# Moving a gate's Silu behind its reload, and loading the Ln/Exp table once for each series of norms

## The chip, the core and the metric

The kernel runs on one core of a Trainium2 chip. The core has five engines, each with its own queue of instructions that it works in order: TensorE (PE in the profile, its weight loads PEld) for matmuls, VectorE (DVE) and ScalarE (ACT) for elementwise work, GpSimd (POOL), and SyncE (SP), which here only issues DMAs. They meet at semaphores. The metric is the device time of one execution in microseconds; the time shown for a kernel is the median of its runs.

## The reference

One layer of a hybrid decoder on x of 1024 tokens by 1024 channels, all in float32: a SwiGLU feed-forward half-step (ffn1), a mixer of three branches (a gated recurrence, sliding-window attention, attention into 256 memory tokens), merged by sigmoid gates and projected, and a second half-step (ffn2). Each has an RMS norm on its input and one on its output.

```python
def rms_norm(x, g):
    xf = x.astype(jnp.float32)
    y = xf * lax.rsqrt(jnp.mean(xf * xf, axis=-1, keepdims=True) + NORM_EPS)
    return (y * g.astype(jnp.float32)).astype(x.dtype)

def swiglu(u, w_in, w_out):
    gate, up = jnp.split(u @ w_in, 2, axis=-1)
    return (jax.nn.silu(gate) * up) @ w_out

f1 = swiglu(rms_norm(h, ffn1_pre_g[l]), ffn1_w_in[l], ffn1_w_out[l])
h = h + HALF_STEP * rms_norm(f1, ffn1_post_g[l])
u = rms_norm(h, mix_pre_g[l])
...
h = h + rms_norm(merged @ w_out[l], mix_post_g[l])
f2 = swiglu(rms_norm(h, ffn2_pre_g[l]), ffn2_w_in[l], ffn2_w_out[l])
h = h + HALF_STEP * rms_norm(f2, ffn2_post_g[l])
```

D_FF is 2816, so gate and up have 22 blocks of 128 columns each.

## The kernel before

**Layout.** Channels lie on the 128 partitions, tokens along the free dimension, in two halves of 512. A float32 operand of a matmul is cut into a high part (a cast, on ACT) and a low part (a subtraction, on DVE), and each product is three matmuls (`mm3`, lines 330 to 332). `split` does this for activations (lines 410 and 411), `operand` for weights (264 and 266). Weights come in strips of 256 KB through five buffers (`w_raw`); eight cut operands (`w_hi`, `w_lo`) are kept ahead of PE.

**Feed-forward input.** The two matrix products are done by a scheme with seven products of quarters of x instead of eight, with seven factors made from them. Two of these factors, `b11` and `b21`, are made from the first half of the tokens alone. So work can begin before the second half is ready:

- the gate phase: for the first 9 blocks of ffn1 and the first 13 of ffn2, `ffn_in_gate` makes the two products with `b11` and `b21`: `px` is copied to `m1` by ACT (line 578), `py` is added to it by DVE (582), and the sum goes through Silu on ACT (583). `m1` and the result `g0` are stored to DRAM (`first_d`, lines 535 and 536).
- beside it, the norm of the second half and the factors made from it (`factors_part`, `factors_end`: lines 498 to 518). In ffn2 this begins with the output norm of the projection, then the input norm of ffn2.
- the pairs (`ffn_in_pair`): for each of the 22 blocks the other five products, with `t2`, `t1`, `t3`, `b22`, `t4`. For the blocks that were begun ahead (called `rest`), `m1` and `g0` are reloaded (595 and 596); the first product `px` plus `m1` gives `u1` (604) and then `px` goes on collecting the third and the fifth product in the same PSUM bank. DVE adds `m1` (625) and multiplies `g0` by the result (626). For the other blocks (called `pair`) `ffn_in_gate` runs inside. Each pair has one more Silu of its own, for the second half of the tokens (621). After each block DVE also makes sums of output weights (552 to 555) and forms of the hidden values (564 to 567), which are stored.

**The norm.** `inverse_root` takes the sum of squares and adds eps while it cuts it in two (`sq_hi` on ACT at 393, `sq_lo` on DVE at 394), loads the table set that holds Ln and Exp (395), lets PE take the mean over the channels (397), and makes the inverse root by Ln (400), Exp (401) and one Newton step: Square on ACT (402), two operations on DVE (403 and 404). It is called 13 times: twice for ffn1's input, four times behind ffn1's output (output norm and mixer norm for each half), four times behind the projection (output norm and ffn2's input norm for each half), and three times at the end (the last half in two pieces).

**Tables.** [...] Silu is not in the set of Ln and Exp. The load at 395 is written out. All others are put in at compile time before an instruction whose function isn't in the set loaded at that point. Casts, copies and Square need no particular set.

**What sets the order.** The queues are filled by a planner that simulates the program: on each engine it takes, among what it holds to be ready, what has the highest priority, which is the order of the program unless `high_priority` moves it up (by `lead` 300 or `urgent` 1000 instructions). `keep` (`keep_in_program_order`) pins an instruction behind the one traced before it on its engine. Once planned, the order on each engine is fixed, and an instruction that waits holds all behind it.

Of the kernel before, what the change touches and what calls it, by code (L numbers as in the profile page):

```python
# [14 lines left out]
ACT = mybir.ActivationFunctionType  # L15
# [192 lines left out]
class Builder:  # L208
# [175 lines left out]
    def inverse_root(self, sq, pool, between=None):  # L384

        nc = self.nc
        n = sq.shape[1]
        hi, lo, y = (pool.tile([P, n], t, tag=f"sq{n}", name=name, bufs=4) for t, name in ((F32R, "sq_hi"), (F32R, "sq_lo"), (F32, "rs")))
        ps = self.psum("ps_rs")[:, :n]
        V, S = nc.vector, nc.scalar  # L390
        keep = self.tc.keep_in_program_order
        with self.tc.high_priority(offset=self.lead):
            keep(S.activation(hi, sq, ACT.Identity, bias=self.eps))
            V.scalar_tensor_tensor(lo, sq, self.eps, hi.bitcast(F32), ALU.add, ALU.subtract)
            keep(S.preload_act_table_set("natural_log_exp_and_others"))
            for i, x in enumerate((hi, lo)):
                mm = nc.tensor.matmul(ps, self.mean_r, x, start=i == 0, stop=i == 1)
                if between:
                    keep(mm)
            keep(S.activation(y, ps, ACT.Ln))  # L400
            keep(S.activation(y, y, ACT.Exp, scale=-0.5))
            keep(S.activation(sq, y, ACT.Square))
            V.scalar_tensor_tensor(sq, ps, -0.5, sq, ALU.mult, ALU.mult)
            V.scalar_tensor_tensor(y, sq, 1.5, y, ALU.add, ALU.mult)
        if between:
            between()
        return y
# [80 lines left out]
    def quarters(self, xs):  # L488
        return ([xs[k + a][h] for k in range(KH)] for h in (0, 1) for a in (0, KH))
# [32 lines left out]
    def ffn_in(self, f, x, form_d, first_d, parts, norm):  # L522

        nc, V = self.nc, self.nc.vector
        with self.tc.tile_pool(reuse_waits="tile", name="ffn_in", bufs=2) as pool:
            self.sums = pool
            self.factors_begin(pool)
            for part in parts:
                norm(part, pool)
                self.factors_part(x, part, pool)  # L530
            self.factors_end(x)

            for j in range(FIRST[f]):
                px, m1, g0 = self.ffn_in_gate(f + "_gate", j, pool)
                nc.sync.dma_start(first_d[j, 0], m1)
                nc.sync.dma_start(first_d[j, 1], g0)
            stored = None
            for i in range(KP):
                *first, made = self.ffn_in_pair(f, 2 * i, pool, first_d)
                self.out_sums(f, i, pool, stored or self.reload, made)  # L540
                *second, _ = self.ffn_in_pair(f, 2 * i + 1, pool, first_d)
                stored = self.out_forms(i, first, second, pool, form_d)
# [26 lines left out]
            stored = nc.sync.dma_start(form_d[B_FORM[n], i], t)  # L569
        return stored  # L570

    def ffn_in_gate(self, name, j, pool):
        nc, fs = self.nc, self.fs
        px, py = self.psum("px"), self.psum("py")
        self.product(px, self.take(name, j), fs["b11"], True)
        x = pool.tile([P, TH], F32, tag="px", name="m1", bufs=3)
        with self.tc.high_priority(offset=self.urgent):
            nc.scalar.copy(x, px)
        self.product(py, self.take(name, j), fs["b21"], True, True)
        g = pool.tile([P, TH], F32, tag="gate", name="g", bufs=6)  # L580
        with self.tc.high_priority(offset=self.urgent):
            nc.vector.tensor_tensor(g, py, x, ALU.add)
        nc.scalar.activation(g, g, ACT.Silu)
        return px, x, g

    def ffn_in_pair(self, f, j, pool, first_d):
        nc, fs = self.nc, self.fs
        V = nc.vector
        ahead = j < FIRST[f]
        name = f + ("_rest" if ahead else "_pair")  # L590
        if ahead:
            px = self.psum("px")
            m1 = pool.tile([P, TH], F32, tag="m1", name="m1", bufs=2)
            g0 = pool.tile([P, TH], F32, tag="gate", name="g", bufs=6)
            self.reload = nc.sync.dma_start(m1, first_d[j, 0])
            nc.sync.dma_start(g0, first_d[j, 1])
        else:
            px, _, g0 = self.ffn_in_gate(name, j, pool)

        def out(ps, what):  # L600
            t = pool.tile([P, TH], F32, tag="px", name=what, bufs=3)
            with self.tc.high_priority(offset=self.lead):
                if ahead:
                    V.tensor_tensor(t, ps, m1, ALU.add)  # L604
                else:
                    nc.scalar.copy(t, ps)
            return t

        pz = self.psum("pz")
        self.product(px, self.take(name, j), fs["t2"], ahead)  # L610
        x = out(px, "u1")
        self.product(pz, self.take(name, j), fs["t1"], True)
        z = out(pz, "m5")
        self.product(px, self.take(name, j), fs["t3"])
        up = pool.tile([P, TH], F32, tag="up", name="up", bufs=2)
        with self.tc.high_priority(offset=self.lead):
            V.tensor_tensor(up, px, z, ALU.add)
        self.product(pz, self.take(name, j), fs["b22"], last=True)
        g1 = pool.tile([P, TH], F32, tag="gate", name="g", bufs=6)
        V.tensor_tensor(g1, pz, x, ALU.add)  # L620
        nc.scalar.activation(g1, g1, ACT.Silu)
        V.tensor_tensor(g1, g1, up, ALU.mult)
        self.product(px, self.take(name, j), fs["t4"], last=True)
        if ahead:
            V.tensor_tensor(m1, m1, px, ALU.add)
            made = V.tensor_tensor(g0, g0, m1, ALU.mult)
        else:
            made = V.tensor_tensor(g0, g0, px, ALU.mult)
        return g0, g1, made
# [915 lines left out]
    def build(self):  # L1545
        nc, tc, io = self.nc, self.tc, self.io
        with contextlib.ExitStack() as outer, tc.tile_pool(reuse_waits="tile", name="consts", bufs=1) as cp, \
             tc.tile_pool(reuse_waits="tile", name="w", bufs=1) as self.wpool, \
             tc.tile_pool(reuse_waits="tile", name="pmm", bufs=8, space=bass.MemoryType.PSUM) as self.pmm:
            self.sum_d = {f: tc.dram_tile([len(SUMS), KP, P, KH, P], F32, name=f + "_sum_d") for f in ("ffn1", "ffn2")}  # L1550
            self.plan()
            self.vecs = cp.tile([P, NVEC], F32, name="vecs")
            nc.scalar.dma_start(self.vecs, io["vecs"])
            self.ones = cp.tile([P, 1], F32, name="ones")
# [40 lines left out]
                    self.mixer_first(u, pool, att_d)  # L1595
            mixed = self.mixer(u, mixc, raws.close, att_d, gate_d, km_d, vm_d)
            consts.close()
            with quarters() as self.qpool:
                merged = self.last_branches(*mixed)
                x = self.acc_tiles()  # L1600
                projection = self.out_projection(merged, x)
                post = lambda part, xr, pool: self.post_norm(x, part, lambda k: self.vec("mix_post_g", k), xr, pool, h2)
                part = next(projection)
                with tc.tile_pool(reuse_waits="tile", name="out_proj", bufs=2) as pool:
                    post(part, self.residual(h1, part, self.res_tile), pool)
                    xr = self.residual(h1, HALVES[1], lambda: self.u_tile(F32))
                    self.factors_norm(x, part, "ffn2_pre_g", pool)
                    self.factors_first(x)

                def ready(part, pool):  # L1610
                    post(part, [t[:, part[1] : part[2]] for t in xr], pool)
                    self.factors_norm(x, part, "ffn2_pre_g", pool)

                self.ffn_in("ffn2", x, form_d, first_d, projection, ready)
                with tc.tile_pool(reuse_waits="tile", name="ffn_out", bufs=2) as pool, \
                     tc.tile_pool(reuse_waits="tile", name="keep", bufs=OPS) as self.keep, \
                     tc.tile_pool(reuse_waits="tile", name="forms", bufs=8) as self.forms:
                    acc = self.new_u()
                    for part in self.ffn_outs("ffn2", form_d, acc):
                        xr = self.residual(h2, part, self.res_tile)  # L1620
                        self.post_norm(acc, part, lambda k: self.post2[:, k : k + 1], xr, pool, io["out"])
# [69 lines left out]
```

## Time and profile before

| | |
|---|---|
| median of 3 runs | 2321.53 us (2320.19 to 2323.29) |
| profiled execution, its own time | 2316.22 us |
| span from first to last instruction | 2314.5 us |
| mean granted PE clock | 0.994 of full speed |
| table loads on ACT at line 395 | 13, of 1283 ns |
| table loads on ACT at line 583 | 5, of 1283 ns |
| Silu at line 583, at line 621 | 44 and 44, of about 632 ns |

A row of a group gives line, engine, operation, output and inputs by name, shapes and count; then busy time in us, mean ns of one, the engine's idle time just before them, and who ended it. A row of a timeline begins with start and duration in us. A row of the waits gives who waited for whom, the total, how often, and the longest. The lines of the functions quoted above are those of the profile.

### The profile page before, as it was taken

The page shows a single profiled execution, that of the slowest core. Times are in us where ns is not written, and L with a number is a line of the kernel's source. Part 1 is how long each engine was busy: PE and PEld are TensorE (multiplying, and loading weights), DVE is VectorE, ACT ScalarE, POOL GpSimd, SP SyncE. Part 2 cuts the span into 40 slices and gives each one's busy share as a digit, 9 for nine tenths or more (in the row PEclk, how much of TensorE's full clock was granted, in tenths as well). Part 3 has the DMA queues.
Part 4 walks back from the last instruction along what each step waited for, and adds up shares of the span by engine and source line. Part 5 has one row for each costly group of instructions (what it writes and reads, how often), then busy time and mean ns, then how long its engine had stood idle before and what let it go on. Part 6 is the DMA issues. An engine that isn't in the chain of part 4 may idle for free. (4 is left out here: it accounts for less than half of the span.)

```text
span 2314.5 us, 33492 instructions
## 1 busy us (share of the span) xinstructions
PE 2263.2 (98%) x11914; PEld 1847.6 (80%) x11914; DVE 1656.0 (72%) x2683; ACT 1008.1 (44%) x1856; POOL 94.9 (4%) x134
## 2 busy tenths in 40 slices
PE   8999999999999999999999999999989999999997
PEld 6778888888888777888878877878868778888887
DVE  6998666665698786995645466575899886666576
ACT  6522333454566553223444454235762223345452
POOL 0000000000000000001300000340000000000000
PEclk9999999999999999999999999999999999999999
DMA  7477544586644447325445334554456774557663
GB/s 271 166 264 249 178 150 168 170 293 201 192 164 156 108 119 193 121 96 180 142 139 176 122 108 151 189 176 168 167 188 233 260 249 167 169 189 268 207 192 118
DMA packets 280776, 417.68 MB, mean 180 GB/s; under 512 B 82304, under 2 KB 104320, under 8 KB 280352
## 3 DMA queue, kind: packets, MB, share of 16 engines
q1 hardware_dynamic: 231552, 388.20, 50.6%
q10 hardware_dynamic: 49056, 27.34, 4.3%
q8 instruction: 94, 1.54, 0.3%
q14 instruction: 74, 0.61, 0.1%
HBM read 284.89 MB, written 129.50 MB: 179 GB/s over the span
## 5 line engine op out<-in xcount | busy, mean ns | idle before, releaser
L264 ACT CAST w_hi<-w_raw 128x512 fp32r<-128x512 f32 x594 | 365.5, 619 | 732.7 <-PE px L331 138.4
L266 DVE TENSOR_TENSOR w_lo<-w_raw,w_hi 128x512 fp32r<-128x512 f32 x594 | 413.6, 699 | 219.3 <-ACT w_hi L264 196.1
L331 PE MATMUL po<-u,w_hi 128*128 128x512 f32 (+1 forms) x476 | 181.0, 380 | 0.0
L330 PE MATMUL po<-u,w_hi 128*128 128x512 f32 (+1 forms) x476 | 181.0, 380 | 0.0
L332 PE MATMUL po<-u,w_lo 128*128 128x512 f32 (+1 forms) x476 | 181.0, 380 | 0.0
L330 PE MATMUL pgate<-u,w_hi 128*128 128x512 f32 x384 | 155.5, 405 | 0.0
L332 PE MATMUL pgate<-u,w_lo 128*128 128x512 f32 x384 | 151.3, 394 | 0.0
L330 PE MATMUL px<-f,w_hi 128*128 128x512 f32 x352 | 139.6, 397 | 11.4 <-DVE u L604 8.6
L331 PE MATMUL pgate<-u,w_hi 128*128 128x512 f32 x384 | 149.8, 390 | 0.0
L330 PE MATMUL px<-u,w_hi 128*128 128x512 f32 x352 | 137.5, 391 | 4.5 <-ACT w_hi L264 2.3
L331 PE MATMUL px<-f,w_hi 128*128 128x512 f32 x352 | 138.2, 393 | 0.3 <-DVE f L411 0.2
L332 PE MATMUL px<-f,w_lo 128*128 128x512 f32 x352 | 137.9, 392 | 0.0
L331 PE MATMUL px<-u,w_hi 128*128 128x512 f32 x352 | 137.0, 390 | 0.8 <-DVE u L411 0.8
L330 PE MATMUL pz<-u,w_hi 128*128 128x512 f32 x352 | 137.1, 390 | 0.2 <-DVE m L604 0.2
L331 PE MATMUL pz<-u,w_hi 128*128 128x512 f32 x352 | 137.2, 390 | 0.0
L332 PE MATMUL px<-u,w_lo 128*128 128x512 f32 x352 | 137.0, 389 | 0.0
L332 PE MATMUL pz<-u,w_lo 128*128 128x512 f32 x352 | 137.0, 389 | 0.0
L411 DVE TENSOR_TENSOR u<-hid,u 128x512 fp32r<-128x512 f32 x114 | 78.3, 689 | 45.2 <-ACT u L410 44.4
L331 PEld LDWEIGHTS po<-u,w_hi 128*128 128x128 f32 x476 | 89.5, 188 | 17.1
L330 PEld LDWEIGHTS po<-u,w_hi 128*128 128x128 f32 x476 | 89.5, 188 | 17.1
L332 PEld LDWEIGHTS po<-u,w_lo 128*128 128x128 f32 x476 | 89.5, 188 | 16.9
L410 ACT CAST u<-hid 128x512 fp32r<-128x512 f32 x114 | 70.7, 620 | 64.9 <-DMA hid<-form_d 56.5
(357 smaller groups left out, 5149.7 us busy)
## 6 DMA issues: line engine op xcount, KB each, us to landing
w_raw<-in_ffn_in SPq DMA_DIRECT2D x220, 256.0 KB
hid<-form_d SPq DMA_DIRECT2D x154, 256.0 KB
w_raw<-in_win SPq DMA_DIRECT2D x112, 256.0 KB
ws<-in_ffn_out SPq DMA_DIRECT2D x88, 256.0 KB
form_d<-g SPq DMA_DIRECT2D x88, 256.0 KB
ffn_sum_d<-ws SPq DMA_DIRECT2D x88, 256.0 KB
w_raw<-ffn_sum_d SPq DMA_DIRECT2D x88, 256.0 KB
form_d<-h SPq DMA_DIRECT2D x66, 256.0 KB
```

Of the source, the lines that this page charges most:

```text
L264: self.nc.scalar.copy(hi, x)
L266: self.nc.vector.tensor_tensor(lo, x, hi.bitcast(F32), ALU.subtract)
L330: mm(out, wh, xh, start=first, stop=False, **kw)
L331: mm(out, wh, xl, start=False, stop=False, **kw)
L332: mm(out, wl, xh, start=False, stop=last, **kw)
L410: self.nc.scalar.copy(hi, x)
L411: self.nc.vector.tensor_tensor(lo, x, hi.bitcast(F32), ALU.subtract)
```

## The change

Two things change. First, the Silu of the blocks begun ahead is no longer made in the gate phase. What is stored in `first_d` is the gate before Silu, and the Silu is made on `g0` after its reload, after the operand of the fifth product has been taken. For the other blocks nothing changes.

Second, a flag `log_table` says whether the set of Ln and Exp has been loaded for the running series of norms. `inverse_root` loads it only if the flag is not set, ahead of `sq_hi` instead of behind it, and sets the flag. The flag is cleared at the start, before the pairs of each feed-forward, and before the last branches of the mixer.

```diff
@@ inverse_root
         with self.tc.high_priority(offset=self.lead):
+            if not self.log_table:
+                keep(S.preload_act_table_set("natural_log_exp_and_others"))
+                self.log_table = True
             keep(S.activation(hi, sq, ACT.Identity, bias=self.eps))
             V.scalar_tensor_tensor(lo, sq, self.eps, hi.bitcast(F32), ALU.add, ALU.subtract)
-            keep(S.preload_act_table_set("natural_log_exp_and_others"))
@@ ffn_in
             for j in range(FIRST[f]):
-                px, m1, g0 = self.ffn_in_gate(f + "_gate", j, pool)
+                px, m1, g0 = self.ffn_in_gate(f + "_gate", j, pool, True)
                 nc.sync.dma_start(first_d[j, 0], m1)
                 nc.sync.dma_start(first_d[j, 1], g0)
             stored = None
+            self.log_table = False
             for i in range(KP):
@@ ffn_in_gate
-    def ffn_in_gate(self, name, j, pool):
+    def ffn_in_gate(self, name, j, pool, early=False):
...
-        nc.scalar.activation(g, g, ACT.Silu)
+        if not early:
+            nc.scalar.activation(g, g, ACT.Silu)
@@ ffn_in_pair
         self.product(px, self.take(name, j), fs["t4"], last=True)
         if ahead:
+            nc.scalar.activation(g0, g0, ACT.Silu)
             V.tensor_tensor(m1, m1, px, ALU.add)
@@ build
             self.plan()
+            self.log_table = False
...
             consts.close()
+            self.log_table = False
             with quarters() as self.qpool:
                 merged = self.last_branches(*mixed)
```

## The prediction

> **What bounds the kernel now.** I read the page first, then the list of who kept TensorE (PE) waiting, then busy times by stretch, and last the timelines of ScalarE (ACT) and VectorE (DVE) around the longest wait. The page's line of engines:
>
> ```profile
> PE 2263.2 (98%) x11914; PEld 1847.6 (80%) x11914; DVE 1656.0 (72%) x2683; ACT 1008.1 (44%) x1856; POOL 94.9 (4%) x134
> ```
>
> PE is busy nearly throughout, so ACT time as such is worth nothing; only places where PE waits can pay. The first of PE's waits (total, times, longest):
>
> ```profile
> PE px L330 <- DVE u L604: 8.6, 2, 8.3
> ```
>
> The one of 8.3 us stands out: a matmul of the third product of the first pair of ffn2 waits for DVE to read the PSUM bank (`u` at L604). Busy times by stretch, in the order PE, PEld, DVE, ACT, POOL, then granted clock, DMA share and GB/s:
>
> ```profile
> 93.00:112.00 19.00, 16.41 (x62) 10.71 (x61) 18.88 (x33) 9.28 (x18) 0.00 (x0) 1.00 0.47 157
> 830.60:834.00 3.40, 0.19 (x1) 0.00 (x0) 0.69 (x1) 2.10 (x4) 0.00 (x0) 1.00 1.04 199
> 835.80:838.80 3.00, 3.00 (x9) 2.33 (x8) 2.74 (x3) 1.36 (x2) 0.00 (x0) 0.50 0.30 119
> ...
> 1691.00:1699.00 8.00, 8.00 (x36) 6.36 (x35) 3.71 (x6) 7.32 (x11) 0.00 (x0) 1.00 0.63 214
> 1699.00:1726.00 27.00, 27.00 (x120) 22.34 (x120) 27.00 (x45) 16.02 (x29) 0.00 (x0) 1.00 0.40 136
> 1726.40:1734.80 8.40, 0.05 (x2) 0.05 (x1) 8.40 (x15) 3.37 (x6) 0.00 (x0) 0.71 0.47 165
> 1734.80:1740.20 5.40, 5.40 (x13) 4.24 (x14) 3.69 (x6) 0.00 (x0) 0.00 (x0) 0.50 0.38 134
> 1745.00:1920.00 175.00, 172.35 (x746) 138.59 (x745) 155.73 (x252) 45.79 (x78) 0.00 (x0) 1.00 0.74 251
> ```
>
> At full speed PE starts 120 matmuls in 27 us, 0.225 us each. In the 8.4 us of the wait it does nothing while DVE is busy all the time, and in the 5.4 us after it the granted clock is 0.50: half of that, 2.7 us, is lost too. The stall costs about 8.3 + 2.7 = 11.0 us. Ffn1 has a smaller likeness at 93 to 112 us: 62 matmuls are worth 14.0 us at 0.225, so 5.0 of the 19 us are lost, with DVE full as well. From 1699 us on DVE has no free moment, so L604 comes when DVE has worked through the second half's norm and factors. But just before, at 1691 to 1699 us, DVE is busy only 3.71 of 8 us while ACT is busy 7.32. ACT there:
>
> ```profile
> 1694.41 0.63 ACT L401 ACTIVATE rs<-rs 128x512 f32<-128x512 f32 x1
> 1695.06 1.28 ACT L583 ACT_TABLE_LOAD   x1
> 1696.36 0.63 ACT L583 ACTIVATE g<-g 128x512 f32<-128x512 f32 x1
> 1696.89 0.57 ACT L578 COPY m<-px 128x512 f32<-128x512 f32 x1
> 1697.36 0.63 ACT L402 ACTIVATE sq<-rs 128x512 f32<-128x512 f32 x1
> ```
>
> Between the norm's Exp (L401) and its Square (L402) stand a gate's Silu, the table load that it needs, and a copy. DVE waits for that Square, here and in the norm before, 5.6 us in two waits (a row of the waits from 1655 to 1740 us):
>
> ```profile
> DVE sq L403 <- ACT sq L402: 5.6, 2, 2.8
> ```
>
> The first of the two waits and what DVE does behind it (the idle time before an instruction stands in brackets):
>
> ```profile
> 1665.44 0.69 DVE L403 SCALAR_TENSOR_TENSOR sq<-ps_rs,sq 128x512 f32<-128x512 f32 x1 [2.79 <-ACT sq L402]
> 1666.05 0.68 DVE L582 TENSOR_TENSOR g<-py,m 128x512 f32<-128x512 f32 x1
> 1666.64 0.68 DVE L404 SCALAR_TENSOR_TENSOR rs<-sq,rs 128x512 f32<-128x512 f32 x1
> ```
>
> **The change, part by part.** *ACT work removed.* The groups of the gates' Silus and of the table loads on ACT, with count, busy time and mean ns:
>
> ```profile
> L583 ACT ACTIVATE g<-g 128x512 f32<-128x512 f32 x44 | 27.7, 632 | 32.5 <-DVE g L582 26.9 <-DMA ffn_sum_d<-ws 5.4
> ...
> L395 ACT ACT_TABLE_LOAD x13 | 16.7, 1283 | 0.2
> ...
> L583 ACT ACT_TABLE_LOAD x5 | 6.4, 1283 | 0.1
> ```
>
> The 13 loads of Ln/Exp become 4 (one for ffn1's input norms, one before its output norms, one in the output projection, one before the last norms). The 5 loads for a gate's Silu become 2, at the first pair of each ffn. Twelve loads of 1.28 us go, 15.4 us of ACT; 22 of the 44 Silus at L583 (9 + 13) move into the pairs. In the load's rows the next instruction starts 1.30 us after it (1695.06 to 1696.36), so I price a load at 1.30. [...]
>
> *Second-half norms of ffn2.* L395's load stands between sq_hi and the Ln, while PE makes the two matmuls of the mean that the Ln needs; I count 0 for it here, and 1.3 us a norm as the other end. The load and Silu ahead of the Square are the price. Without them the Square can follow the Exp: at 1695.04 instead of 1697.36, 2.3 us sooner. The norm before has the same shape:
>
> ```profile
> 1661.83 0.63 ACT L401 ACTIVATE rs<-rs 128x512 f32<-128x512 f32 x1
> ...
> 1664.77 0.63 ACT L402 ACTIVATE sq<-rs 128x512 f32<-128x512 f32 x1
> ```
>
> 1662.46 instead of 1664.77, again 2.3 us. Both come out of DVE's idle time, and DVE's load up to L604 is unchanged, so L604 should come 4.6 us sooner: the wait falls from 8.3 to about 3.7 us. Should the copy stay ahead of each Square (0.47 us from its start to the Square's), it is 3.7 us.
>
> *The clock after it.* At 830.6 us PE stood still for 3.4 us and then had clock 0.50 in a stretch of 3.0 us, a loss of 1.5 us. That row is nearest to a wait of 3.7 us, so the cold stretch shrinks from 2.7 to 1.5 us of loss and saves 1.2; the ends are 0 and 2.7. Ffn2 together: 4.6 + 1.2 = 5.8 us.
>
> *Second-half norm of ffn1*, the Exp and the Square there:
>
> ```profile
> 60.65 0.63 ACT L401 ACTIVATE rs<-rs 128x512 f32<-128x512 f32 x1
> ...
> 63.59 0.63 ACT L402 ACTIVATE sq<-rs 128x512 f32<-128x512 f32 x1
> ```
>
> 61.28 instead of 63.59, 2.3 us once more, against 5.0 us that PE loses at 93 to 112. Some may go to waits for weights on the way; I take 2.0, between 0 and 2.3.
>
> *The last norm.* Here the load does hold the Ln; the mean's second matmul on PE, then ACT:
>
> ```profile
> 2302.24 0.38 PE L397 MATMUL ps_rs<-sq_lo,mean_r 128*128 128x256 f32 x1
> ```
>
> ```profile
> 2301.68 1.28 ACT L395 ACT_TABLE_LOAD   x1
> 2302.98 0.38 ACT L400 ACTIVATE rs<-ps_rs 128x256 f32<-128x256 f32 x1
> ```
>
> The sum is there at 2302.62, Ln could start some 0.06 us later: 0.3 us saved, at the very end of the chain.
>
> *Loads ahead of sq_hi.* The four that stay now stand before L393, behind the last square of the sum. In the projection:
>
> ```profile
> 1604.19 0.63 ACT L420 ACTIVATE sq<-acc 128x512 f32<-128x512 f32 x1
> 1605.59 0.72 ACT L393 ACTIVATE sq_hi<-sq,eps 128x512 fp32r<-128x512 f32 x1 [0.76 <-DVE sq L424]
> ```
>
> 1604.82 + 1.30 is 1606.12, 0.5 us after sq_hi starts now, and PE's matmul of the mean follows it. I charge 0.5 us in all; at worst it is 0.5 at each of the three later ones, 1.5.
>
> *Silu in the pairs.* 22 times about 0.53 us (its pitch at 1696.36 to 1696.89), at the end of a pair behind the reload `g<-first_d` (L596). For the second pair of ffn2, the issue on the SP queue, and the product on DVE that uses it:
>
> ```profile
> 1745.76 0.42 SPq L596 DMA_DIRECT2D g<-first_d  x1
> ```
>
> ```profile
> 1766.63 0.69 DVE L626 TENSOR_TENSOR g<-g,m 128x512 f32<-128x512 f32 x1
> ```
>
> The reload has 21 us. ACT is busy 45.8 of the 175 us from 1745 on, which covers the Silus and the one Silu table load per ffn; I put them at 0. Without that cover each Silu would stand ahead of a weight cast (L264) that PE needs. No DMA is added. The stores of `g` in the gate phase leave the SP queue sooner, since they no longer wait for the Silu; what is queued behind them is weight loads, and I count nothing for that.
>
> *Sum.* -5.8 - 2.0 - 0.3 + 0.5 = -7.6 us against the profiled execution's 2316.22 us, that is 2308.6. That execution lies 5.3 us under the median of the runs, 2321.53, so on the median's footing 2321.5 - 7.6 = **2314 us**. What is late next in ffn2 is still L604, by 3.7 us.
>
> **The rivals.** *DVE's order eats the gain.* DVE works its queue in order, and behind L403 at 1665.44 stands L582 for a gate, whose product PE finishes at its own pace. If the order stays and that product is no older than L582's start at 1666.05, L404 stays at 1666.64 and the first norm gains nothing; ffn1 has the same program. For it: this is how the queue is ordered now. Against it: the order is planned anew with the loads gone. If all three norms lose their gain so, 0.3 us at the end and 0.5 of charges are left: about 2321.7 us, 2321 with a little of the second norm's.
>
> *The clock stays up.* If the wait falls a little further, the granted clock need not drop, and the whole 2.7 us come back: 1.5 more than the forecast, 2312.5 us. For it: a wait of 3.7 us is close to the 3.4 us at 830 us; against it: that one did drop the clock. [...]
>
> *Silus on PE's path.* Slower: in the pairs DVE is busy 155.7 of 175 us, and the weights go through ACT's cast, DVE's subtraction, and PE. A Silu put ahead of a late cast, or waiting there for its reload with the casts behind it, delays PE. At its full 0.63 us in all 22 pairs that is 13.9 us, less 7.6: 2328 us. It cancels the gain from 0.35 us a pair and makes the kernel slower by 0.2% from 0.55. Against it: ACT is idle three quarters of that stretch.
>
> **How the numbers follow.** Forecast 0.50 (own range 2310 to 2318), clock stays up 0.12, order eats the gain 0.24, Silus on the path 0.14. The range of 2309 to 2323 us holds the first three nearly whole: its low end is the whole clock loss and ffn1's 2.3 with no charge at all (4.6 + 2.7 + 2.3 + 0.3 = 9.9) and 2 to 3 us for Ln's loads (above) and the runs' spread; its high end is the second rival's 2321 with the other 1.0 us of charges. About 0.2%, 4.6 us, is what a measurement of this kernel can tell from no change. Faster by more, under 2316.9: 0.46 of the forecast's 0.50, and 0.12, so 0.58; the same: 0.04 and 0.24, so 0.28; slower: 0.14.
>
> **What would show it.** Six table loads of these two kinds in the profile after instead of 18. L402 right behind L401, and L403's wait for it well under 2.8 us, in the three second-half norms. The wait for L604 at about 3.7 us, with a cold stretch of some 3 us behind it; at 8 us the order has eaten the gain. The losses at 93 to 112 us down by about 2. In the pairs the same waits of PE as now: waits for `w_hi` that grow there would make the prediction wrong, as would a wait of ACT for `g<-first_d`.

## The result, and the profile after

The median falls from 2320.43 to **2312.53 us** (six runs each, 2309.42 to 2317.92 after): a ratio of 0.9971 [0.9961, 0.9981], 7.9 us. On a second occasion it was 2312.15 against 2319.88 us, 0.9961 [0.9947, 0.9974]; against a second set of the kernel before on that occasion (2317.37, eleven runs) the medians lie 5.2 us apart.

A warning first: runs of one kernel differ by several microseconds (21 of the kernel before lay between 2314.43 and 2324.76), and a trace shows one run. The traced run shown above took 2316.22 us, 4 under its kernel's median; the traced run of the changed kernel took 2317.92, 5 over its own. Taken alone, the pair would show a loss. So each kernel was traced again ("second trace": 2320.14 us before, 2311.74 after), and where a stage is compared, both are given.

The page of the changed kernel, its line of engines:

```profile
PE 2263.1 (98%) x11914; PEld 1848.4 (80%) x11914; DVE 1657.5 (72%) x2683; ACT 995.3 (43%) x1844; POOL 94.5 (4%) x134
```

ACT has 12 instructions fewer (1856 before) and 12.8 us less to do; PE's busy time is the same to 0.1 us. The groups of the loads and the moved Silus on ACT (count, then busy time, mean ns, idle time before them and who ended it):

```profile
L629 ACT ACTIVATE g<-g 128x512 f32<-128x512 f32 x22 | 13.9, 631 | 22.8 <-DMA g<-first_d 16.6 <-DMA ffn_sum_d<-ws 5.1 <-DMA w_raw<-in_ffn_in 1.0
...
L394 ACT ACT_TABLE_LOAD x4 | 5.1, 1283 | 0.1
...
L629 ACT ACT_TABLE_LOAD x2 | 2.6, 1283 | 5.4 <-DMA g<-first_d 5.4
```

Four loads of Ln and Exp and two for a Silu, as announced. The last numbers of the first and third row were not announced: ACT stands still before the moved Silus, 28 us in all, 22 of them for the reload (16.6 and 5.4). In the second half's norm of ffn2, Exp (now L403) and Square (L404) on ACT, first trace after:

```profile
1692.04 0.63 ACT L403 ACTIVATE rs<-rs 128x512 f32<-128x512 f32 x1
1692.70 0.63 ACT L404 ACTIVATE sq<-rs 128x512 f32<-128x512 f32 x1
```

0.66 us apart instead of 2.95. DVE's waits for it from 1655 to 1740 us:

```profile
DVE sq L405 <- ACT sq L404: 1.0, 2, 0.5
```

It was 5.6. And of PE's waits over the whole span, four rows (total, times, longest; the two larger ones, at other places, are nearly as before: 7.0 us against 7.1 and 6.0 against 5.6):

```profile
PE ps_rs L399 <- ACT sq_hi L396: 5.4, 7, 2.0
PE pz L330 <- DVE m L608: 5.2, 1, 5.2
PE px L330 <- DVE up L621: 4.8, 8, 1.3
PE px L330 <- DVE u L608: 3.1, 2, 2.8
```

The 8.3 us behind `u` in ffn2's first pair are gone (the 2.8 in the last row are in ffn1). In the same pair PE now waits 5.2 us for `m`, the other result of the same line, one product further. The stretches of that wait and of what follows it (PE, PEld, DVE, ACT, POOL, then granted clock, DMA share, GB/s):

```profile
1730.00:1738.00 8.00, 2.80 (x13) 2.03 (x12) 7.12 (x12) 4.49 (x9) 0.00 (x0) 0.92 0.30 103
1737.60:1743.50 5.90, 5.76 (x14) 4.59 (x15) 5.06 (x9) 2.70 (x5) 0.00 (x0) 0.50 0.31 104
```

So the stall has become shorter and has moved, and the cold stretch (matmuls at half clock, 0.50 in the second row) behind it is no shorter than before. Stage lengths in us, from the first matmul into `pz` of one stage to that of the next (`pz` takes the second product of a pair). For ffn1 the first column begins with the first gate and holds the gate phase and what PE does ahead of the first `pz`, the second the nine pairs begun ahead; for ffn2 the first pair and the other twelve begun ahead:

```
                          ffn1            ffn2              median of
                          gates  pairs    first  other 12   the runs
before, two traces        57.4   132.3    24.8   174.9      2320.43
                          56.8   132.8    23.7   177.1
after, two traces         54.0   135.9    22.1   175.5      2312.53
                          53.5   134.5    21.1   174.3      2312.15
```

In ffn1 this mark does not cut both kernels at the same work: before, 20 matmuls into `px` stand between the last gate and the first `pz`, after, 12. So only the sum of its two columns can be compared from kernel to kernel (189.7 and 189.6 before, 189.9 and 188.0 after). Counted by matmuls instead, in us from the first gate's first matmul to the start of the given one (the gates have 216, the nine pairs 540):

```
                          217th   325th   517th   757th
before, two traces        50.6    80.4    126.6   181.5
                          50.1    79.8    125.6   181.4
after, two traces         51.3    77.4    124.3   181.8
                          50.8    77.6    123.5   179.8
```

The gate phase itself is 0.7 us longer. The changed kernel gets 3.0 and 2.2 us ahead in the first pairs; at the end of the nine, all of that is lost again in the first trace and 0.6 us in the second.

### The profile page after: what moved, and what is told of

Same layout as the page of the kernel before. It is cut to its first block, busy times and chain, and to the rows that moved or that the text cites. A ratio compares the mean times of both kernels' runs of the same rounds, so it can differ in the third digit from the quotient of the medians.

```text
span 2316.2 us, 33482 instructions
## 1 busy us (share of the span) xinstructions
PE 2263.1 (98%) x11914; PEld 1848.4 (80%) x11914; DVE 1657.5 (72%) x2683; ACT 995.3 (43%) x1844; POOL 94.5 (4%) x134
## 5 line engine op out<-in xcount | busy, mean ns | idle before, releaser
L332 PEld LDWEIGHTS po<-u,w_lo 128*128 128x128 f32 x476 | 89.5, 188 | 17.1
```

The lines of the kernel that those rows point to most:

```text
L332: mm(out, wl, xh, start=False, stop=last, **kw)
```

## The experiments

Theory A: the gain comes from the three second-half norms, where Silu and table load stood between Exp and Square. Rival B: it comes a little at a time from all the loads that are gone. The first four kernels ran on one chip.

**The two kernels again.**

> The kernel before, unchanged, for a second trace and for what two runs of one kernel differ by. All theories: ratio 1.000 within 0.001; the stall of about 8.3 us of PE behind L604 in ffn2 again, the same stage lengths within 1 us; stages that differ by more are where this kernel scatters.

> The changed kernel once more, beside the kernel before on the same chip, for an interval and a second trace. Theory A (the gain comes from the three second-half norms, where Exp and Square now follow each other): 7 to 9 us under the kernel before, the gate phases and the first pairs together 6 to 8 us shorter. Rival B (the gain is spread over all norms, a fraction of a load at each): as much in the sum, but the gate phases and first pairs hold less than half of it.

Before: 2317.37 us in its own runs, ratio 0.999 [0.9981, 0.9999] to the 21 shared runs, those of the same kernel that the first four kernels are all compared with. So 0.1% is within the scatter of this comparison. The stall is there again; the stages scatter by more than the 1 us named, ffn2's twelve later pairs by 2.2. After: the time is as expected against the shared runs. The place is not: counted by equal matmuls, the gate phases and first pairs are shorter by 3.5 us together in the second traces (1.1 in ffn1, 2.4 in ffn2) and by 4.5 in the first, not by 6 to 8. That is about half the gain, so this run alone does not tell A from B.

**The Silu moved alone.** Every norm loads for itself, behind `sq_hi`.

```diff
-            if not self.log_table:
-                keep(S.preload_act_table_set("natural_log_exp_and_others"))
-                self.log_table = True
             keep(S.activation(hi, sq, ACT.Identity, bias=self.eps))
...
+            keep(S.preload_act_table_set("natural_log_exp_and_others"))
```

> Only the first half of the change: the Silu of the gates begun ahead moves behind its reload; every norm still loads its own table behind sq_hi (13 loads of Ln/Exp, 2 for a gate's Silu). Theory A: nearly the whole gain, 6 to 8 us under the kernel before, since this alone takes Silu and table load from between Exp and Square. Rival B (loads of the table as such cost): 9 of the 12 loads are still there, so at most a third of the gain, 2 to 3 us.

> The Silu moved alone, each norm loading its table behind sq_hi, a second time beside the others: for a second trace and on one chip with the raised priority. Expected 9 to 12 us under the kernel before; ffn2's first pair 16 to 17 us again with no cold stretch behind it. If the raised priority equals it within 1.5 us, the order of m5 was all that set the changed kernel behind it.

2309.06 us, ratio 0.9945 [0.9933, 0.9958], and on the second occasion 2310.69, 0.9949 [0.9937, 0.996]. Half the change gives no less than the whole, by the medians 2 to 3 us more, though the intervals overlap: B falls, and A does not say why. The DVE timeline of both kernels at the place of the stall does. The changed kernel, second trace (idle time in brackets):

```profile
1724.86 0.68 DVE L608 TENSOR_TENSOR u<-px,m 128x512 f32<-128x512 f32 x1
1726.44 0.69 DVE L266 TENSOR_TENSOR w_lo<-w_raw,w_hi 128x512 fp32r<-128x512 f32 x1 [0.90 <-ACT w_hi L264]
...
1732.46 0.69 DVE L608 TENSOR_TENSOR m<-pz,m 128x512 f32<-128x512 f32 x1
```

The Silu moved alone:

```profile
1721.92 0.71 DVE L605 TENSOR_TENSOR u<-px,m 128x512 f32<-128x512 f32 x1
1722.87 0.69 DVE L605 TENSOR_TENSOR m<-pz,m 128x512 f32<-128x512 f32 x1 [0.24 <-PE pz L332]
```

Here the planner has put `m` right behind `u`; in the changed kernel ten rows stand between them, splits of factors and of weights and two sums of weights. PE's waits in that pair with the Silu moved alone (from 1715 to 1740 us):

```profile
PE px L330 <- DVE up L618: 2.4, 1, 2.4
```

One wait of 2.4 us, a granted clock of 1.00 behind it, and a first pair of 16.5 us in both traces, as expected the second time.

**The table loaded once, the Silu left in the gate phase.**

```diff
-            if not self.log_table:
+            early = not self.log_table and not self.mixed_silu
+            if early:
                 keep(S.preload_act_table_set("natural_log_exp_and_others"))
                 self.log_table = True
             keep(S.activation(hi, sq, ACT.Identity, bias=self.eps))
...
+            if self.mixed_silu:
+                keep(S.preload_act_table_set("natural_log_exp_and_others"))
```

> Only the second half of the change: the table is loaded once for each series of norms, but the gates' Silu stays in the gate phase, and the norms beside the gates therefore still load for themselves (7 loads of Ln/Exp, 5 for a gate's Silu). Theory A: 0 to 1 us under the kernel before (0.3 at the last norm less the charges for loads ahead of sq_hi); the stall of 8.3 us in ffn2 unchanged. Rival B: about half the gain, 3 to 5 us.

2316.41 us, ratio 0.9984 [0.9975, 0.9994], where the kernel before itself had 0.999 [0.9981, 0.9999]: no gain beyond that comparison's scatter can be told. B's 3 to 5 us are met only against the shared runs of before, not against the kernel's own second set. A's "stall unchanged" was missed: it is 6.3 us, because in the second of the two norms the new plan has put the Square ahead of the Silu and its load:

```profile
1696.47 0.63 ACT L406 ACTIVATE rs<-rs 128x512 f32<-128x512 f32 x1
1697.00 0.61 ACT L264 CAST w_hi<-w_raw 128x512 fp32r<-128x512 f32 x1
1697.51 0.63 ACT L407 ACTIVATE sq<-rs 128x512 f32<-128x512 f32 x1
1698.16 1.28 ACT L591 ACT_TABLE_LOAD   x1
```

Every edit draws a new plan; that had to be separated next.

**The order of `m` mended, in all pairs begun ahead.**

```diff
         def out(ps, what):
-            with self.tc.high_priority(offset=self.lead):
+            with self.tc.high_priority(offset=self.urgent if ahead else self.lead):
```

> The changed kernel with one priority raised: in the pairs begun ahead, DVE's additions u1 and m5 (L608) go ahead of the remaining splits of the factors. In the planned order of ffn2's first pair, m5 then stands 4 places behind u1 instead of 11. Theory A (what is left of ffn2's stall is the order of m5 behind the splits): the wait of 4.6 us for m5 falls under 1.5, no cold stretch behind it, ffn2's first pair lasts 16 to 17 us instead of 21 to 22, and the time is 3 to 6 us under the changed kernel, 10 to 13 under the kernel before. Rival B (the changed kernel is behind the kernel with the Silu moved alone because its loads stand ahead of sq_hi): the first pair may change, but the time stays within 2 us of the changed kernel's 2312.

2315.35 us, ratio 0.9973 [0.9963, 0.9983]. At the place itself theory A holds in part: no wait for `m`, one of 2.4 us for `up` instead, a first pair of 17.7 us in place of the 16 to 17 named, and a cold stretch of 2.6 us is still there (granted clock 0.90 over the pair). But the time is not lower, because ffn1's pairs take 139.6 us in place of 134.5 and 135.9, with two new cold stretches (granted clock 0.53 from 127.9 to 131.5 and from 175.7 to 179.3 us). So the next kernel has it only where it is needed.

**The same in ffn2's first pair alone.**

```diff
-            with self.tc.high_priority(offset=self.lead):
+            with self.tc.high_priority(offset=self.urgent if name == "ffn2_rest" and j == 0 else self.lead):
```

> The changed kernel with the priority of u1 and m5 (L608) raised in the first pair of ffn2 alone; everywhere else the priorities are those of the changed kernel. Theory (the raised priority helped in ffn2's first pair, 17.7 us instead of 21 to 22, and lost it again in the pairs of ffn1): ffn1's pairs begun ahead last as in the changed kernel, 133 to 136 us together, ffn2's first pair 16 to 18 us, no cold stretch behind it, and the time is 3 to 5 us under the changed kernel, 2307 to 2310. Rival (what the raised priority lost was the scatter of the runs): 2315 again.

**2307.43 us** (2305.42 to 2309.58), ratio 0.9952 [0.9938, 0.9966]: 11.5 us under the kernel before. Against the changed kernel (0.9971 and 0.9961) it is better by 2 to 4 us, by ratios taken on different occasions whose intervals overlap. Ffn1's pairs last 132.6 us, ffn2's first 17.9. The only wait of PE there (1718 to 1740 us), and the clock behind it:

```profile
PE px L330 <- DVE up L621: 2.6, 1, 2.6
```

```profile
1730.00:1733.00 3.00, 2.89 (x7) 2.32 (x8) 3.00 (x7) 2.31 (x5) 0.00 (x0) 0.50 0.06 23
```

"No cold stretch" was missed. With `m` in its place the whole change equals the Silu moved alone (0.9952 against 0.9945 and 0.9949): loading the table once adds nothing that these runs can tell. In ffn2's first pair the order of `m` accounts for what set the changed kernel behind (21.1 and 22.1 us against 17.9); in the time the difference is of the size of the intervals.

**The same priority in the kernel before.** The same edit at L604, Silu and loads where they were.

> The kernel before with the priority of u1 and m5 (L604) raised in the first pair of ffn2 alone: the Silu and its table loads stay between Exp and Square. It asks whether the stall in ffn2 needs the change at all, or only DVE's order. In the planned order u1 and m5 now stand ahead of 9 of the 10 splits that stood ahead of them. Theory F (order alone): the wait of 8.3 us falls to 2 to 3 us, ffn2's first pair lasts 18 to 20 us as in the changed kernel with the same priority, and the time is 4 to 6 us under the kernel before. Theory G (DVE's backlog): DVE still reaches its last split 6 us later, so PE waits for the splits or for `up` instead, the first pair stays at 22 to 25 us and the time within 2 us of the kernel before. Ffn1 should show no change by either.

2320.23 us against 2324.4, ratio 0.9986 [0.9975, 0.9997]. The first pair lasts 24.2 us by its 60 matmuls (22.0 by the mark at `pz`, which comes early here: 2 matmuls of the second pair stand ahead of it and not 12), against 24.8 and 23.7 before. `u` runs 8 us sooner, and PE waits for what was pushed behind it (1720 to 1765 us):

```profile
PE pz L330 <- ACT w_hi L264: 2.5, 1, 2.5
PE px L331 <- DVE f L411: 1.3, 1, 1.3
```

with cold stretches of 2.6 and 5.1 us (granted clock 0.51 in both). G holds for the stage; the time, 3.2 us under by the ratio, lies between the two. But in the first comparison the unchanged kernel too lay 0.1% under the shared runs, and the stage shows no gain, so the order alone yields nothing sure here; the gain needs the norms to end sooner as well.

**The load against the Silu's own time.** The Silu stays behind the reload, and a copy of the gate onto itself takes its place in the gate phase.

```diff
-        if not early:
+        if early:
+            nc.scalar.activation(g, g, ACT.Copy)
+        else:
             nc.scalar.activation(g, g, ACT.Silu)
```

> The changed kernel with an ACT copy of the gate onto itself in the gate phase, where the Silu stood: the same ACT time as the Silu (about 0.6 us each, 22 times), but no table load. It tells the load from the Silu in the three norms. If the load between Exp and Square is the price (1.30 of 2.3 us a norm) and the Silu's own 0.5 us the smaller rest: ffn2's factors begin 1 to 1.5 us later than in the changed kernel, against 6.2 us in the kernel before, and the time lies 5 to 11 us under the kernel before (its planned order has m5 directly behind u1). If the ACT time as such were the price, half of the 6.2 us would be back, and the time at 3 to 5 us under.

2315.51 us, ratio 0.9967 [0.9954, 0.998], 5.4 us. The factors in ffn2 begin 1.0 us later than in the changed kernel, as expected of the load. ACT in the first norm:

```profile
1663.05 0.64 ACT L403 ACTIVATE rs<-rs 128x512 f32<-128x512 f32 x1
1663.58 0.62 ACT L587 ACTIVATE g<-g 128x512 f32<-128x512 f32 x1
1664.10 0.62 ACT L404 ACTIVATE sq<-rs 128x512 f32<-128x512 f32 x1
```

The copy sits where the Silu sat and holds the Square by 0.4 us against 2.3 with the load. Its first pair takes 17.1 us by its 60 matmuls, with no cold stretch, but the other twelve 179.3 instead of 174 to 176; why was not followed up. (The mark at `pz` comes early here too and gives 14.9 and 181.5.)

**The moved Silus left out.** The mended order of the first try, without the 22 Silus.

```diff
         if ahead:
-            nc.scalar.activation(g0, g0, ACT.Silu)
             V.tensor_tensor(m1, m1, px, ALU.add)
```

> As the kernel with the raised priority, but the Silu of the reloaded gates is left out altogether (22 Silus, and with them the two table loads in the first pairs; the output is not the layer's). It measures what the Silus cost in the pairs. Forecast (hidden beside PE): within 1.5 us of the kernel with the raised priority, and the same stage lengths in the pairs within 1 us. Rival (Silus on PE's path): 22 x 0.35 to 0.63 us = 8 to 14 us shorter in the pairs begun ahead.

2310.73 us, ratio 0.9951 [0.9939, 0.9963], 4.6 us under the kernel it was set against. That misses the forecast of 1.5, but it is the other kernel that had the odd ffn1. Against the two kernels that keep the Silus and have `m` in order (0.9952 and 0.9949) nothing is gained, and the twelve later pairs of ffn2 take 175.8 us with no Silus and 176.0 with them. The rival's 8 to 14 us are excluded. Other than expected, the two table loads have not gone with the Silus: they stand ahead of the pairs' own Silu now.

**Twenty DMAs fewer in ffn1.** The stores of the first five blocks' weight sums are left out in both kernels, whose output is then not the layer's.

```diff
         for n, t in zip(SUMS, (a22, a11, a21, a12)):
-            nc.sync.dma_start(self.sum_d[f][SUMS.index(n), q], t)
+            if f == "ffn2" or q >= 5:
+                nc.sync.dma_start(self.sum_d[f][SUMS.index(n), q], t)
```

> The kernel before without 20 of the DMAs in ffn1's first pairs: the sums of output weights of the first five blocks are made on DVE but not stored, and where they would be loaded later the strips they were made from are loaded (the output is not the layer's). It is the base for the changed kernel with the same DMAs left out. Theory D (the weights' transfers set the time in ffn1's pairs begun ahead): its pairs begun ahead last 2 us or more less than before's 132 to 133. Theory E (DVE's order sets it): the same length within 1 us.

> The changed kernel without the same 20 DMAs in ffn1's first pairs. Theory D (ffn1 gives back half of its 3.3 us because the weights' transfers do not come sooner): with room on the queue the head start stays, and the first pair that is not begun ahead starts 3 us or more sooner than in the kernel before with the same DMAs left out. Theory E (it is DVE's order): it starts 1 to 2 us sooner, as with all DMAs (230.2 against 228.4 us in one pair of traces).

2316.49 us (0.9992 [0.9983, 1.0002]) and 2311.49 us (0.9969 [0.9956, 0.9982]). From the first gate to the first pair not begun ahead it is 190.0 and 187.1 us: 2.9 us, just short of D's 3. But the kernel before did not get shorter by them (132.6 us in its pairs), which is E's forecast. Neither theory is borne out as a whole, and one trace of each does not settle it.

## Why the prediction came out right, and where its steps did not

The forecast was 2314 us, 7.6 under the median; 7.9 and 7.7 were measured. The sum was better than its terms: the two places that it named hold 4.2 of the 7.7 us in the second traces and 2.5 of the 7.9 in the first, so that the total came out is in part luck. The starts of DVE's instructions in ffn2, counted from PE's first matmul of the gate phase (the second traces, the first of the two kernels agree within 0.9 us; L403, the operation behind the Square, is L405 in the changed kernel):

```
                            before   after    Silu alone  mended in first pair
L403, first norm            16.88    13.62    14.21       13.63
L403, second norm           49.43    41.88    42.98       41.83
factors begin               58.34    52.14    53.21       52.07
u of the first pair         85.41    76.90    77.26       75.99
m of the first pair         87.81    84.51    78.21       79.28
```

*Second-half norms of ffn2.* The mechanism was right and the term too small: the factors begin 6.2 us sooner, not 4.6. Of it 2.7 and 2.3 lie between `sq_lo` and L403 in the two norms, against 2.3 each as priced; 2 more come between the two norms and 0.6 ahead of the first, 1.3 is lost again behind the second.

*The price of a load, and 0 for L395's load behind `sq_hi`.* Both hold. Where the row behind a load waits for nothing else, it starts 1.29 to 1.30 us after the load does (1659.01 to 1660.30 in the first trace before, 1728.41 to 1729.71 in the first after), and the Silu moved alone, which keeps that load, reaches L403 as fast from `sq_lo` (3.76 us in the second norm) as the changed kernel (3.75).

*L604 4.6 us sooner, the wait falls from 8.3 to 3.7.* This step failed. It took DVE's queue up to L604 as unchanged. `u` came 8.5 us sooner: the factors began 6.2 us sooner, and the new plan put six of their last splits ahead of it where eleven stood. And `m`, which had had three rows of DVE between `u` and itself, now had ten; it came only 3.3 us sooner. The rival "DVE's order eats the gain" saw that the order could, but put the loss at L404.

*The clock after it.* The step failed in kind: I let the cold stretch shrink with the wait. Waits of 5.2 and 4.6 us were each followed by 5.1 us at half clock (0.50 and 0.51; from the first to the last start of a slow matmul), the 8.3 before by 4.7 and 2.5. Ffn2's first pair is therefore shorter by 2.6 us from one second trace to the other (2.7 from first to first), not by 5.8. With `m` in place it is 6 to 8. The rival "clock stays up" came true only in the kernels with the Silu moved alone, left out (granted clock 1.00 over the first pair of both), or with a copy in its place.

*Ffn1.* The term is borne out where it was read: at the 325th matmul the changed kernel is 3.0 and 2.2 us ahead, against 2.0 in the sum and 2.3 as its bound. But that it would last to the end of the pairs is not: 1.6 us are left there in the second traces and none in the first. What is late next there is a transfer. DVE in the kernel before, second trace:

```profile
161.29 0.69 DVE L285 TENSOR_TENSOR w_sum<-w_raw 128x512 f32<-128x512 f32 x1 [0.80 <-DMA w_raw<-in_ffn_in]
```

and in the changed kernel:

```profile
161.18 0.69 DVE L285 TENSOR_TENSOR w_sum<-w_raw 128x512 f32<-128x512 f32 x1 [1.32 <-DMA w_raw<-in_ffn_in]
```

PE is 2.3 us ahead at this point (the 517th matmul starts at 166.2 us before and at 163.9 after), yet the strip lands at the same time. DMA share from 160 to 172 us, changed kernel:

```profile
160.00:172.00 12.00, 11.14 (x49) 8.75 (x48) 10.49 (x18) 3.44 (x6) 0.00 (x0) 1.00 0.94 318
```

That transfers hold it there is what these rows say; the experiment with fewer stores did not confirm it.

*The last norm and the loads ahead of `sq_hi`.* From `sq_hi` to Ln the last norm takes 1.76 and 1.56 us instead of 1.82 in both: 0.1 to 0.3 us, as priced. PE's waits for `sq_hi` grew from 4.4 and 3.8 us to 5.4 and 4.9: about 1.0 where I charged 0.5, within the 1.5 of the bound.

*Silus in the pairs at 0.* Right for the later pairs, by the kernel without them. Wrong in what would show it: ACT does wait for `g<-first_d`. I had read the reload's 21 us off the second pair and taken them for all; in the first pair it is issued while the gate phase still stores. ACT there, second trace after:

```profile
1723.97 1.28 ACT L629 ACT_TABLE_LOAD   x1 [3.40 <-DMA g<-first_d]
1725.27 0.63 ACT L629 ACTIVATE g<-g 128x512 f32<-128x512 f32 x1
1725.80 0.60 ACT L264 CAST w_hi<-w_raw 128x512 fp32r<-128x512 f32 x1
```

The cast behind it is the one that DVE waits 0.90 us for, between `u` and `m` above. The rival "Silus on PE's path" had this very mechanism. ACT waits for the reload 13 and 15 times in the two traces, 22.0 and 23.5 us, but casts stand still behind it only twice and once, for 2.0 and 0.4 us; in ffn2's first pair it costs under 2 us (16.0 us without the Silus, 17.7 and 17.9 with them, the clock's share included).

*Where the rest of the sum is.* By the second traces ffn1 gives 1.6 us and ffn2's first pair 2.6, by the first traces less; the other 3 to 4 of the 7.7 us I cannot place. All other stages differ by 1 to 2 us between traces of one kernel, so two traces do not show it. Against the second set of the kernel before, where the gain is 5.2 us, only 1 us would be left to place. The granted clock over all runs of the second occasion gives a hint: its mean is 0.9933 in 21 runs before and 0.995 in 5 after, which over 2315 us is an estimated 4 us less lost to half clock. In which stretches that is stays open: the four traces do not show it (0.9939 and 0.9944 before, 0.9943 and 0.9946 after).

## What to carry to other kernels

Here a table load between two dependent ACT instructions put its 1.3 us into the wait of DVE for the second (with the Silu behind it, 5.6 us in two norms against 1.0 without both), so look for a load in the consumer's wait and not in ACT's share of the span. Where a planner fixes the queues, an edit that frees time also redraws the order: list what stands ahead of the late instruction after the edit, and set the order of the two or three instructions that matter; here that took 3 to 4 us off the first pair of ffn2, and the gain by the medians went from 7.7 to 11.5 us. Raise the priority only where it is needed, and judge differences of a few microseconds by medians, since one trace of each kernel can show the opposite sign.

## What the runs showed of the hardware

Behind one and the same wait of about 2 us the clock dropped in some traces and not in others. In every trace PE waits 2.16 to 2.19 us for the same ACT instruction (`raw`) at about 878 us (2.47 in the kernel with the copy). The 3.3 us behind it in the kernel before, first trace:

```profile
878.00:881.30 3.30, 3.30 (x15) 2.71 (x16) 2.75 (x3) 0.62 (x3) 0.00 (x0) 1.00 1.00 303
```

and second trace:

```profile
878.70:882.00 3.30, 3.30 (x9) 2.57 (x10) 2.83 (x3) 0.62 (x3) 0.00 (x0) 0.58 0.97 296
```

15 matmuls against 9, after the same wait. Of the 13 traces with that wait, 5 show the drop, the first of the changed kernel among them behind 2.16 us, a shorter wait than the 3.4 us at 830 us from which the prediction argued. All waits of 3.4 us and more behind PE's first matmul were followed by a drop, whose length went from 2.1 to 5.5 us without regard to the wait's (4.7 and 2.5 us behind 8.3, 5.1 behind 5.2). So here the wait brought from 8.3 to 5.2 us saved no more than the wait (the first pair became 2.7 us shorter in the first traces), and each such wait cost an estimated 1 to 3 us beyond itself (half of 2.1 to 5.5 us).
